# Rows of the split tokens: from one place modulo 256 bytes per tile to places that alternate from row to row

## The chip, the cores and the metric

The kernel runs on one core of a Trainium2 chip. A core has TensorE (matrix products; the profile's PE, with PEld for its weight loads), VectorE (DVE), ScalarE (ACT), GpSimd (POOL) and SyncE (SP, which here only issues transfers). The metric is the device time of one execution in microseconds (us), as the median of several runs. SBUF is the core's working memory: 128 partitions, in each of which a tile takes a run of bytes. A "place" below is the byte address of a row within its partition, modulo 256.

## What is computed

One layer of a decoder trunk over 4096 prompt tokens and 64 sample tokens, width 1024. Cut to what matters:

```python
h = _rmsnorm(x, g_pre)
z = h @ w_in                       # (tokens, 1024) @ (1024, 2816)
cb, cc, ch, cg, q, k, v, ag, mq, mg = _split_cols(z)
out_a = silu(cg) * cb * conv3(cc * ch)           # gated short convolution
out_b = silu(ag) * window_attention(q, k, v)     # window 128, a sink per head
out_c = silu(mg) * memory_attention(mq)          # 256 memory tokens
y = concat([out_a, out_b, out_c]) @ w_out
x = x + _rmsnorm(y, g_post)
```

All in float32, and the outputs also hold the new keys, values and convolution states. The change concerns the product `h @ w_in` alone.

## The kernel before, in words

The kernel has two long stages: the input projection (to about 917 us), then attention, output projection and the last norm, block by block.

**The input projection.** The 4160 tokens go in 8 blocks of 2 x 260 tokens (`HW = 260`). Three phases (`PHASES`) take 4, 4 and 3 pairs of 128-column groups of `w_in`, and in each phase all blocks run through. In the first phase the two first blocks (`PLAIN_BLOCKS`) are computed directly, in 8 steps; all others by a Strassen-Winograd scheme of 7 products per pair (`PRODUCTS`), each on a token operand (B.., T..) and a weight operand (A.., S..) that are sums of quarters. A token operand is a tile of 128 partitions x 4 rows (`KH = 4`, the parts of the contraction) x 260 tokens.

**Splitting.** TensorE multiplies in a reduced form of float32 (`F32R`), so every operand is split into a rounded part and the rest: `split` (line 363 on ScalarE, line 364 on VectorE) makes `hi` and `lo` of a token operand, `x_split` does so for the plain blocks, `w_split` for the weights, which lie as `w[:, 0]` and `w[:, 1]` in one tile of 2 x 512 columns.

**The product.** `product` (line 373) runs 12 matmuls of 128 x 260 into one PSUM bank: for each of the 4 rows k, `hi[k]` with the weights' first half, `lo[k]` with the same weights, `hi[k]` with the second half. The token row is the moving operand, the 128 x 128 piece of weights is loaded before each matmul. The sequence of moving rows is thus hi, lo, hi, then hi, lo, hi of the next row. The result is moved out of PSUM by `evict` (VectorE, ScalarE), and the `finish_...` functions store it to DRAM for the second stage.

**Where the split tiles lie.** `hi` and `lo` have two buffers each, from one pool `hp`, made after the pool `hx` of the unsplit operands. A tile has 4 rows of `XR = 320` elements of 4 bytes, 1280 bytes, five times 256; 260 of the 320 are used, from element 48 on in `hi` and from element 16 on in `lo` (`begins`). As the program is built, the `lo` buffers begin at 131680 and 136800, the `hi` buffers at 141920 and 147040. So every used row of `lo` lies at place 160 and every row of `hi` at place 32. The pieces of weights lie at place 224, all of them.

**What sets the order.** In the first stage the program fixes the order of work by hand on every engine (`manual_schedule`); the order doesn't depend on where tiles lie. When the second stage opens (`open_attention`), the pools of the first are closed and their bytes are given to new tiles; whoever first writes such a tile waits for the last user of the bytes.

Of the kernel before, what the change touches and what calls it, by code (L numbers as in the profile page):

```python
# [8 lines left out]
F32 = mybir.dt.float32  # L9
F32R = mybir.dt.float32r  # L10
# [5 lines left out]
P = 128  # L16
D = 1024
KT = D // P
KH = KT // 2
# [2 lines left out]
NB = 8  # L22
NT = 4096 + NS
HW = 260
XR = 320
NBLK = NT // (2 * HW)
CT = 256
NCH = 4096 // CT
# [19 lines left out]
def f(ap):  # L48
    return ap.bitcast(F32)
# [3 lines left out]
def hybrid_layer(ctx: ExitStack, tc: tile.TileContext, a: dict):  # L53
# [31 lines left out]
    pa = ExitStack()  # L85
# [2 lines left out]
    psa = ExitStack()  # L88

    place = ctx.enter_context(tc.tile_pool(name="place", bufs=1)).tile([P, 2, KH, HW], F32, name="place")  # L90
    hxp = pa.enter_context(tc.tile_pool(name="hx", bufs=4))
    hp = pa.enter_context(tc.tile_pool(name="hp", bufs=2))
    own = ExitStack()
    kept_z = ExitStack()
    zp, used = {}, {1: [], 2: []}
# [37 lines left out]
    def accumulator(i, w, name):  # L133

        tag = "xy"[i % 2]
        if pa1 is None:
            return pa2[tag].tile([P, 2, 512], F32, tag=tag, name=name)
        return pa1[tag, w].tile([P, w, 512], F32, tag="c", name=name)
# [212 lines left out]
                tc.keep_in_program_order(ins)  # L351
            store(hd[b][o], ops[o])

    begins = {"hi": 48, "lo": 16}

    def split_tile(tag, name):

        n = begins[tag]
        return hp.tile([P, KH, XR], F32R, tag=tag, name=name)[:, :, n : n + HW]

    def split(src, name):
        hi, lo = split_tile("hi", f"hi{name}"), split_tile("lo", f"lo{name}")
        S.copy(hi, src)
        V.tensor_tensor(lo, src, f(hi), op=ALU.subtract)
        return hi, lo
# [216 lines left out]
    def x_split(b, o, meanwhile=lambda: None):  # L582
        x = xs[0, b][o]
        h0[b, o] = hi, lo = [split_tile(n, f"{n}0_{b}{o}") for n in ("hi", "lo")]
        for k in range(KH):
            if k == 1:
                meanwhile()
            g = gain_of(o, k)
            S.mul(hi[:, k], x[:, k], g)
            V.scalar_tensor_tensor(lo[:, k], x[:, k], g, f(hi[:, k]), op0=ALU.mult, op1=ALU.subtract)  # L590
# [112 lines left out]
    x_of(0, 0, "B21")  # L703

    idle = accumulator(1, 2, "idle")
    warm = hp.tile([P, KH, XR], F32R, tag="lo", name="warm").rearrange("p k n -> p (k n)")
    G.memset(f(warm[:, : P + 512]), 1.0)
    for n in (416, 416, 416, 416, 512, 512, 512, 416):
        TE.matmul(idle[:, 0, :n], warm[:, :P], warm[:, P : P + n], start=True, stop=True)
# [980 lines left out]
```

## Time and profile before

| | |
|---|---|
| time, median of 3 runs | 1530.43 us (1530.04 to 1531.11) |
| the profiled execution | 1529.03 us, span 1527.3 us |
| matmuls of the input projection, line 373 | to about 917 us |
| attention and output projection | from about 917 us on |
| DMA, mean over the span | 201 GB/s, 306.28 MB |

The profile is one execution. Its page gives busy times by engine, the chain of work that ended last, and groups of instructions by source line; other views list the busy time in chosen stretches, the waits, and the instructions in order of time. Two things are to be kept in mind. A matmul's end is modelled and matmuls overlap, so the mean duration of a row is not the distance from one to the next; that distance is found by counting matmuls in a stretch without waits. And a few matmul records can be missing, so counts come from the code where they matter.

### The profile page before, as it was taken

What the parts mean: (1) busy time and instruction counts of PE and PEld (TensorE: products, weight loads), DVE (VectorE), ACT (ScalarE), POOL (GpSimd) and SP (SyncE); (2) the same over time, 40 slices, a digit from 0 to 9 for tenths busy, and PEclk for the clock granted to TensorE, in tenths of its full rate; (3) what the DMA queues carried; (4) which work ended last, traced back from release to release, by engine and by line L of the source; (5) the groups of instructions that cost most, each with busy time, mean ns of one, the idle gap of its engine ahead of it and who ended that gap; (6) DMA issues with size and microseconds to landing.
All of it is one profiled execution on the core that took longest, in us unless ns stands there. A gap on an engine that the chain in (4) does not pass through costs nothing.

```text
span 1527.3 us, 30150 instructions
## 1 busy us (share of the span) xinstructions
PE 1514.2 (99%) x11331; PEld 1391.6 (91%) x11331; DVE 1145.1 (75%) x2055; ACT 806.2 (53%) x2039; POOL 381.0 (25%) x604
## 2 busy tenths in 40 slices
PE   9999999999999999999999999999999999999998
PEld 9999999999999999999999998788888888888876
DVE  6778888899887777997677678766666666666743
ACT  7776666576222222445455457656655565565632
POOL 0222333221300000000101204544444444444310
PEclk9999999999999999999999999999999999999999
DMA  9989999878755333778877789977777777776333
GB/s 274 200 213 242 286 277 259 301 238 273 194 182 181 127 127 127 240 231 278 243 262 224 242 286 259 226 160 149 149 148 152 162 149 158 162 155 145 131 110 97
DMA packets 177943, 306.28 MB, mean 201 GB/s; under 512 B 33926, under 2 KB 107654, under 8 KB 177766
## 3 DMA queue, kind: packets, MB, share of 16 engines
q1 hardware_dynamic: 130901, 227.38, 48.2%
q0 software_dynamic: 46176, 75.92, 24.9%
q8 instruction: 90, 1.47, 0.4%
q10 hardware_dynamic: 720, 1.05, 0.2%
q14 instruction: 56, 0.45, 0.1%
HBM read 197.23 MB, written 108.05 MB: 200 GB/s over the span
## 4 chain that ended last, share of the span: by engine, by line
PE 87%; DVE 5%; issue 4%; DMA 2%; POOL 1%; ACT 1%; SPq 0%; ACTq 0%; POOLq 0%; DVEq 0%
PE c L373 47%; PE y L1499 23%; PE ws L1253 4%; PE wo L1095 2%; PE wt L1276 2%; PE xs L1189 2%; PE xt L1204 2%; PE wo L1225 2%; PE wo L1231 1%; PE mem_acc L796 1%; DVE z L380 1%; DMA ws10A<-in_w_in 1%; DMA vd<-v 1%; DMA place<-hd_B 0%; DMA ws20A<-in_w_in 0%
## 5 line engine op out<-in xcount | busy, mean ns | idle before, releaser
L1499 PE MATMUL y<-wo,mh 128*128 128x512 f32 (+1 forms) x1040 | 350.1, 399 | 0.0
L380 DVE TENSOR_TENSOR z<-c,z 128x520 f32<-128x520 f32 (+1 forms) x308 | 194.8, 647 | 80.7 <-PE c L373 79.0
L1499 PEld LDWEIGHTS y<-wo,mh 128*128 128x128 f32 x1040 | 194.3, 188 | 39.3 <-issue 2.4
L1499 PE MATMUL y<-wo,ml 128*128 128x512 f32 (+1 forms) x520 | 201.8, 388 | 0.0
L1266 ACT ACTIVATE sm<-sm,wnm 128x128 f32<-128x128 f32 x256 | 99.5, 390 | 60.9 <-DVE wnm L1260 60.0
L1198 POOL TENSOR_SCALAR xp<-xp,xrd 128x256 f32<-128x256 f32 x128 | 74.6, 590 | 208.0 <-DVE xrd L1194 207.1
L1499 PEld LDWEIGHTS y<-wo,ml 128*128 128x128 f32 x520 | 98.2, 189 | 16.2
L1190 DVE TENSOR_REDUCE xmx<-xs 128x2 f32<-128x512 f32 x64 | 44.1, 689 | 59.3 <-PE xs L1189 59.2
L1278 ACT COPY wpt<-wt 128x512 f32<-128x512 f32 x64 | 37.2, 582 | 87.7 <-PE wt L1276 85.2
L1253 PEld LDWEIGHTS ws<-kst,q 128*128 128x128 f32 x512 | 70.0, 190 | 5.4 <-ACT xp L1193 0.7
L1506 DVE TENSOR_TENSOR yn<-y,gpost 128x512 f32<-128x512 f32 (+1 forms) x66 | 45.1, 684 | 39.6 <-PE y L1499 39.3
L1253 PE MATMUL ws<-kst,q 128*128 128x256 f32 x512 | 73.1, 283 | 0.4 <-ACT xp L1193 0.4
L1507 ACT ACTIVATE y<-y 128x512 f32<-128x512 f32 (+1 forms) x66 | 38.5, 584 | 64.2 <-DVE yn L1506 64.2
L744 POOL CAST wmask<-negs 128x256 uint8<-128x256 f32 x1 | 0.8, 822 | 265.2 <-ACT z L382 265.2
L1286 POOL TENSOR_SCALAR_AFFINE_SELECT wpt<-wpt 128x512 f32<-128x512 f32 x64 | 52.7, 823 | 42.0 <-ACT wpt L1278 39.1
L1193 ACT ACTIVATE xp<-xs,xnm 128x256 f32<-128x256 f32 x128 | 58.9, 464 | 7.1 <-DVE xnm L1191 7.1
L1128 POOL DMA_DIRECT2D q<-qd x64 | 42.8, 674 | 70.2 <-DMA qd<-zh 60.2
L1117 POOL DMA_DIRECT2D kst<-qd x64 | 38.7, 617 | 63.7 <-PE xt L1204 41.5
L1517 DVE SCALAR_TENSOR_TENSOR xr<-yn,yst,xr 128x1024 f32<-128x1024 f32 (+2 forms) x34 | 43.1, 1269 | 14.6 <-POOL yst L1513 13.2
L1256 DVE COPY_PREDICATED sm<-wmask,ws 128x256 f32<-128x256 uint8 x124 | 52.1, 436 | 2.4 <-ACT sm L1255 2.0
L1283 POOL TENSOR_SCALAR_AFFINE_SELECT wpv<-wpt 128x512 f32<-128x512 f32 x62 | 40.5, 653 | 50.6 <-ACT wpt L1278 50.5
L275 ACT ACTIVATE nat<-nat 104x1024 f32<-104x1024 f32 x40 | 42.3, 1057 | 18.5 <-DMA nat<-in_x_p 18.5
(962 smaller groups left out, 5076.2 us busy)
## 6 DMA issues: line engine op xcount, KB each, us to landing
q<-qd POOLq DMA_DIRECT2D x64, 384.0 KB, 8.3
xr<-in_x_p SPq DMA_DIRECT2D x32, 512.0 KB
nat<-in_x_p SPq DMA_DIRECT2D x39, 416.0 KB
o_yp<-xr SPq DMA_DIRECT2D x31, 512.0 KB
md<-th POOLq DMA_DIRECT2D x48, 260.0 KB, 7.2
qd<-zh SPq DMA_DIRECT2D x48, 260.0 KB
qd<-z SPq DMA_DIRECT2D x48, 260.0 KB
kst<-qd POOLq DMA_DIRECT2D x60, 192.0 KB, 5.5
```

Of the source, the lines that this page charges most:

```text
L373: TE.matmul(bank[:, :HW], l, r, start=first and i == 0, stop=last and i == 3 * KH - 1)
L380: add = lambda dst, other: V.tensor_tensor(dst, c, other, op=ALU.add)
L1190: V.tensor_reduce(mx[:, :nb], s, axis=AX.X, op=ALU.max)
L1193: S.activation(p[:, i, :], s[:, i, :], AF.Exp, bias=nm[:, i : i + 1], scale=SCALE, accum_out=den[:, i : i + 1])
L1198: G.tensor_scalar(p[:, i, :], p[:, i, :], rd[:, i : i + 1], 0.5, op0=ALU.mult, op1=ALU.mult)
L1253: TE.matmul(s3[:, hh, :], self.q[:, 4 + 2 * (2 * half + hh) + kvh, i * P : i * P + P], self.kst[:, 2 * kvh + part, i * P : i * P + 2 * P], ...
L1256: V.copy_predicated(sm[:, 2 * half : 2 * half + 2, :], third["wmask"], third["negs"] if first else s3[:, :, 0:P])
L1266: S.activation(sm[:, hh, :], sm[:, hh, :], AF.Exp, bias=nm[:, hh : hh + 1], scale=SCALE, accum_out=den[:, hh : hh + 1])
L1286: G.affine_select(p3, p3, pattern=[[0, 4], [1, P]], compare_op=ALU.is_ge, fill=0.0, base=0, channel_multiplier=-1)
L1499: TE.matmul(acc, self.hl[l][:, k], wo[k][c0 // 512][:, r, c0 % 512 : c0 % 512 + c1 - c0], start=j == 0, stop=j == passes * KT - 1)
L1506: V.tensor_tensor(yn[:m, c0:c1], acc[:m], gpost[:m, c0:c1], op=ALU.mult)
L1517: V.scalar_tensor_tensor(self.xr[:m, cs], yn[:m, cs], st[:m, 3:4], self.xr[:m, cs], op0=ALU.mult, op1=ALU.add)
```

## The change

Rows are 288 elements apart in place of 320, 1152 bytes, which is four and a half times 256. `hi` and `lo` get a pool each, `lo` first, and two small tiles that nothing uses (64 and 128 bytes) stand ahead of them. The rows begin at the start of the tile.

```diff
-XR = 320
+XR = 288
...
+    pads = [0]
+
+    def pad(where, n):
+
+        pads[0] += 1
+        where.enter_context(tc.tile_pool(name=f"pad{pads[0]}", bufs=1)).tile([P, n], F32, name=f"pad{pads[0]}")
+
     hxp = pa.enter_context(tc.tile_pool(name="hx", bufs=4))
-    hp = pa.enter_context(tc.tile_pool(name="hp", bufs=2))
+    pad(pa, 16)
+    hp = {"lo": pa.enter_context(tc.tile_pool(name="hplo", bufs=2))}
+    pad(pa, 32)
+    hp["hi"] = pa.enter_context(tc.tile_pool(name="hphi", bufs=2))
...
-    begins = {"hi": 48, "lo": 16}
-
     def split_tile(tag, name):
 
-        n = begins[tag]
-        return hp.tile([P, KH, XR], F32R, tag=tag, name=name)[:, :, n : n + HW]
+        return hp[tag].tile([P, KH, XR], F32R, tag=tag, name=name)[:, :, :HW]
...
-    warm = hp.tile([P, KH, XR], F32R, tag="lo", name="warm").rearrange("p k n -> p (k n)")
+    warm = hp["lo"].tile([P, KH, XR], F32R, tag="lo", name="warm").rearrange("p k n -> p (k n)")
```

As the program is built, the `lo` buffers begin at 131744 and 136352 (place 160) and the `hi` buffers at 141088 and 145696 (place 32). The places of the moving rows in one product are then:

| k, matmul | before | after |
|---|---|---|
| 0: hi, lo, hi | 32, 160, 32 | 32, 160, 32 |
| 1: hi, lo, hi | 32, 160, 32 | 160, 32, 160 |
| 2: hi, lo, hi | 32, 160, 32 | 32, 160, 32 |
| 3: hi, lo, hi | 32, 160, 32 | 160, 32, 160 |

Every engine has the same instructions in the same order as before. The tiles that lie behind the split tiles in the first stage (z tiles, temporaries, row factors) come to lie 1856 bytes lower or, in the second and third phase, elsewhere by a similar amount, at other places modulo 256; the weights and the tiles of the second stage stay. At the opening of the second stage the waits for released bytes change for a few instructions: the first writers of the tiles over the former place of z tiles wait for partly other stores of the projection's last block.

## The prediction

> **What bounds the kernel.** I read the page's busy shares first, then the windows view by stage, then the waits of TensorE, then the matmul rows of one undisturbed stretch.
>
> ```profile
> PE 1514.2 (99%) x11331; PEld 1391.6 (91%) x11331; DVE 1145.1 (75%) x2055; ACT 806.2 (53%) x2039; POOL 381.0 (25%) x604
> PEclk9999999999999999999999999999999999999999
> PE c L373 47%; PE y L1499 23%; PE ws L1253 4%; PE wo L1095 2%; PE wt L1276 2%; PE xs L1189 2%; PE xt L1204 2%; PE wo L1225 2%; PE wo L1231 1%; PE mem_acc L796 1%; DVE z L380 1%; DMA ws10A<-in_w_in 1%; DMA vd<-v 1%; DMA place<-hd_B 0%; DMA ws20A<-in_w_in 0%
> ```
>
> TensorE is busy 99% of the span at full granted clock, and the chain that ended last runs mostly through its matmuls: first those of line 373, the only ones the change touches. The windows view (stretch, its length, then busy time and count of PE, PEld, DVE, ACT, POOL, clock, DMA share, GB/s) and the waits of PE and PEld show how tight that is:
>
> ```profile
> 112.00:343.00 231.00, 231.00 (x1964) 231.00 (x1962) 201.94 (x251) 144.23 (x252) 65.22 (x107) 1.00 0.93 265
> 343.00:640.00 297.00, 294.44 (x2490) 293.40 (x2489) 246.19 (x336) 98.55 (x130) 20.49 (x20) 1.00 0.54 176
> 640.00:917.00 277.00, 277.00 (x2281) 270.98 (x2281) 210.14 (x334) 135.78 (x245) 22.30 (x34) 1.00 0.79 256
> PE idle L709 <- POOL warm L707: 2.2, 1, 2.2
> PE c L373 <- DVE lo_2T L364: 0.9, 2, 0.5
> PE c L373 <- DVE lo_3T L364: 0.9, 1, 0.9
> PE c L373 <- DVE lo_0B L364: 0.7, 1, 0.7
> PE c L373 <- ACT hi_3T L363: 0.2, 1, 0.2
> PE c L373 <- DVE lo_0T L364: 0.2, 1, 0.2
> ```
>
> Up to 917 us, where the products of line 373 end, line 373 waits 2.9 us in all (0.9 + 0.9 + 0.7 + 0.2 + 0.2). VectorE has 29 us to spare in the first of these stretches (231.00 - 201.94) and 51 us in the second. So what a matmul of line 373 gains or loses in spacing arrives almost whole at the end of the span. The question is only whether the spacing changes.
>
> **How the matmuls are spaced.** The code issues 64 + 168 + 224 + 168 = 624 products (two plain blocks of 8 x 4, six of 7 x 4, eight of 7 x 4, eight of 7 x 3) of 12 matmuls each: 7488. The first row below is the windows view of PE alone over 140 us without a wait; the others are line 373 in 12 us of the same stretch (minimum/median/maximum in ns).
>
> ```profile
> 480.00:620.00 140.00, 140.00 (x1191) 1.00 0.34 118
> L373 PE MATMUL c<-hi_5B,w_1A x16: 281/282/282, 540.5 to 547.5; 128*128 128x260 f32 x16
> L373 PE MATMUL c<-hi_5B,w_2A x16: 281/282/282, 541.9 to 548.9; 128*128 128x260 f32 x16
> L373 PE MATMUL c<-lo_5B,w_1A x8: 277/278/278, 540.7 to 547.4; 128*128 128x260 f32 x8
> L373 PE MATMUL c<-lo_5B,w_2A x8: 277/278/278, 542.1 to 548.8; 128*128 128x260 f32 x8
> ```
>
> The 1191 matmuls that touch the window started within 140.28 us (it also catches those begun up to 0.28 us earlier): **117.8 ns** from start to start. The rows' durations overlap, and run about 163 ns above the spacing, so differences between them stand for differences in spacing to within a nanosecond or so. Every row is 128x260, weights are 128x128 throughout, and yet a matmul on `hi` lasts 282 ns and one on `lo` 278. Two things differ between them. One is the place: `hi` rows all start at 32 modulo 256, `lo` rows all at 160, weights always at 224. The other is the neighbour: `hi`, `lo`, `hi` and then `hi` again means that one step in three, 2496 of 7488, goes from a row to another at the same place.
>
> That columns alone don't set the spacing is seen beside it, in the page's row of the score product, whose moving rows have 256 columns and keep one place within each block:
>
> ```profile
> L1253 PE MATMUL ws<-kst,q 128*128 128x256 f32 x512 | 73.1, 283 | 0.4 <-ACT xp L1193 0.4
> 400.66 0.19 PEld L373 LDWEIGHTS c<-hi_1T,w_3S 128*128 128x128 f32 x1
> 400.78 0.28 PE L373 MATMUL c<-hi_1T,w_3S 128*128 128x260 f32 x1
> 400.78 0.19 PEld L373 LDWEIGHTS c<-hi_1T,w_0S 128*128 128x128 f32 x1
> 400.89 0.28 PE L373 MATMUL c<-hi_1T,w_0S 128*128 128x260 f32 x1
> ```
>
> Four columns fewer, 283 ns: no shorter. The timeline under it shows why that is possible: the weights for the next matmul begin to load as the current one starts, and 0.11 us later the next starts. Loading and streaming run side by side, both reading SBUF. My reading is that the two reads get into each other's way by a few ns, by an amount that depends on where the moving row lies. The row shows no collision; it is an inference from 282 against 278.
>
> **The change, part by part.** Nothing is added, removed or reordered on any engine; sizes of all operations are the same. Three things move.
>
> *Places of the split rows.* After it, of the 12 matmuls of a product 6 read at 32 and 6 at 160 (before: 8 and 4), no step stays at one place, and 12 is even, so the alternation carries on into the next product. Two ways to count:
> - If the place decides: 7488 x (8/12 - 6/12) = 1248 matmuls go from 282 to 278 ns, -1248 x 4 = **-5.0 us**.
> - If the step decides: the 2496 same-place steps go from the upper `hi` value, 282, to the mean of the other two kinds, (281 + 278) / 2 = 279.5, which is -2.5 x 2496 = **-6.2 us**. That the 282s among the `hi` rows are the same-place steps is assumed.
>
> The two share a mechanism and differ by 1.2 us; I take the middle, **-5.6 us**. The far bound of a gain: all 2496 steps reach 278, -10.0 us. The bound of a loss is the 120 ns rhythm below.
>
> *Everything behind the split tiles in SBUF* (z tiles, temporaries) moves down by up to 1856 bytes and to other places modulo 256. The DVE evictions, ACT copies and DMAs keep their shapes. Only VectorE and ScalarE rows carry this, and they have the slack named above; I take 0, between -1 and +1 us. If that slack were gone the 0.9 us waits on `lo` would grow with each block, 22 blocks by some tenths.
>
> *Waits at the opening of the attention stage.* Its tiles lie over released ones, and a few first writers, above all the copies into `xpt`, now wait for the last store of `zh` as well:
>
> ```profile
> 930.30 1.11 SPq L165 DMA_DIRECT2D qd<-zh  x1
> 941.53 0.38 ACT L1208 COPY xpt<-xt 128x256 f32<-128x256 f32 x1
> md<-th POOLq DMA_DIRECT2D x48, 260.0 KB, 7.2
> ```
>
> It is issued at 930.30 + 1.11 = 931.4; a store of the same size lands a median 7.2 us later, at 938.6, and the copy is at 941.53: 2.9 us of cover. If a shorter first stage leaves these distances alone, as it should, this costs 0; if the store took 3 us longer, up to that.
>
> **Sum.** -5.6 + 0 + 0. The profiled run took 1529.03 us for a span of 1527.3; it becomes 1523.4. It lies 1.4 below the median of the three runs, 1530.43, so I forecast the median at 1530.43 - 5.6 = **1524.8 us**.
>
> **The rivals.**
>
> *The rhythm locks at 120 ns.* Line 373 has a second steady rhythm. From 772 us on, without any wait:
>
> ```profile
> 773.02 0.28 PE L373 MATMUL c<-hi_3T,w_1S 128*128 128x260 f32 x1
> 774.46 0.28 PE L373 MATMUL c<-hi_3T,w_2S 128*128 128x260 f32 x1
> L373 PE MATMUL c<-lo_3B,w_0S x4: 281/281/281, 782.2 to 783.3; 128*128 128x260 f32 x4
> L373 PE MATMUL c<-hi_3B,w_0S x8: 282/282/284, 782.1 to 783.4; 128*128 128x260 f32 x8
> ```
>
> The first two rows are the first matmuls of two products in a row: 1.44 us for 12, 120 ns each, and in this state `lo` lasts 281. Same code, same places: which rhythm holds depends on how loading and streaming stand to each other when the stretch begins, and a stretch stays in it until a wait breaks it. It is rare now. If the new alternation makes it the one that holds everywhere, the price is 7488 x (120 - 117.8) = +16.5 us: **1546.9 us**, slower. It decides from the first steady product on. For it: the score product's 283 ns are like this state's 282 and 281, so a rhythm of this kind can hold for long. Against it: in the score product the places don't alternate, and in line 373 it is the alternating `lo` steps that are short; with more of them the short rhythm should hold better, not worse. Chance 0.18.
>
> *The place plays no part.* `lo` is also the only matmul that is followed by a load from the other half of the weight tile (`w[:, 1]`); if that makes its 278, nothing changes: **1530.4 us**. The rows can't exclude it, since role and place never come apart in this kernel. The Trainium skill speaks for this one: its page "TensorE: Matmul & The Clock Gate", in the section "Step-by-step: what each phase is for", gives TensorE two independent SBUF read ports, one for the moving operand and one for the weights, and under "Back-to-back issue gap" a spacing of N / 2.4 + 2.5 ns, in which no place occurs; by it 260 columns would take an estimated 110.8 ns and this change would do nothing. The trace's 117.8 ns, and two durations for one shape, don't agree with that spacing. Chance 0.20.
>
> *A larger gain.* All steps fall to the short value: -10.0 us, **1520.4 us**. Chance 0.07, since a step to `lo` lasts 281 today.
>
> **How the numbers follow.** Forecast 0.55, larger gain 0.07, no part 0.20, 120 ns rhythm 0.18. About 0.2%, 3 us, is what a measurement of this kernel tells from no change. Faster: 0.55 + 0.07 = 0.62; same 0.20; slower 0.18. The range takes in the far gain and the case of no change with the +1 and up to 3 us of the two small terms, 1519.5 to 1533.5; the slow rhythm, 0.18, is left out. The forecast's own range, with the step from 5.0 to 6.2 us and the small terms, is 1522 to 1527.
>
> **What would show it.** In the new profile, 480 to 620 us should hold 1197 to 1199 matmuls in place of 1191 (140.28 us / 117.2 to 117.0 ns, the spacing less 5.0 or 6.2 us / 7488). The groups of line 373 tell the reasons apart: if the place or the step decides, `hi` and `lo` rows each mix 278 with 281 or 282, and their medians no longer differ by role; if role decides, `lo` stays at 278 and `hi` at 282; if the slow rhythm holds, both lie at 281 to 284 and the window has about 1169 (140.28 us / 120 ns). The start of line 1499 should come some 5 us earlier, and the attention stage from 917 us to the end should last as long as now. A changed time in that stage, or waits of `c` on `lo` that grow over 3 us, would make the working wrong even where the total fits.

## The result, and the profile after

The changed kernel is slower. Its median is 1536.86 us (15 runs, 1534.41 to 1544.69), beside 1531.52 us of the kernel before (15 runs, 1529.17 to 1536.44). The ratio, taken over all the runs, is **1.0043, 95% interval 1.0031 to 1.0054**: 0.0043 x 1531.52 = 6.6 us lost (the two medians alone are 5.3 us apart), where 5.6 us of gain was forecast.

The profiled execution took 1537.16 us for a span of 1535.4, 8.1 us more than the span before, which is at the upper end of that interval (0.0054 x 1531.52 = 8.3). The first three lines are of the page (busy times, granted clock, chain that ended last):

```profile
PE 1522.6 (99%) x11331; PEld 1400.7 (91%) x11331; DVE 1145.3 (75%) x2055; ACT 806.6 (53%) x2039; POOL 379.3 (25%) x604
PEclk9999999999999999999999999999999999999999
PE c L380 55%; PE y L1506 23%; PE ws L1260 4%; PE wo L1102 2%; PE wt L1283 2%; PE xs L1196 2%; PE xt L1211 2%; PE wo L1232 2%; PE wo L1238 1%; PE mem_acc L803 1%; DMA qd<-z 1%; DMA xr<-in_x_p 0%; DMA ws20A<-in_w_in 0%; DVE z L387 0%; DVE wo L195 0%
```

Line 373 is now line 380, and line 1499 is 1506. TensorE is busy 8.4 us longer (1522.6 - 1514.2) with as many instructions at the same clock; VectorE, ScalarE and GpSimd kept their busy times within 2 us. What is lost is lost inside TensorE's own work. The windows view (stretch, its length, busy time and count of PE, PEld, DVE, ACT and POOL, clock, DMA share, GB/s), cut at the end of the first stage, and the output product by source line (minimum/median/maximum in ns, first and last start) say in which stage:

```profile
0.00:923.00 923.00, 918.90 (x7605) 910.76 (x7606) 738.98 (x1047) 459.94 (x786) 128.72 (x198) 1.00 0.76 228
923.00:1535.40 612.40, 603.71 (x3729) 489.89 (x3727) 406.30 (x1010) 346.66 (x1255) 250.56 (x406) 1.00 0.71 157
L1506 PE MATMUL y<-wo,mh x1040: 277/393/504, 931.3 to 1528.9; 128*128 128x512 f32 x168, 128*128 128x256 f32 x6
```

The same view of the kernel before has its first output product at 924.0 us and its last at 1520.8. So the first comes 7.3 us later, and from the first to the last it is 597.6 us now and 596.8 before: about 0.8 us of the 8.1 lies in the second stage, the rest in the first. The other profiles have 595.9 to 598.6 us for the same stretch, so that 0.8 us is no more than these differ among themselves. Two windows without a wait, PE alone, before and then after, show the spacing:

```profile
490.00:620.00 130.00, 130.00 (x1106) 1.00 0.32 112
490.00:620.00 130.00, 130.00 (x1096) 1.00 0.33 116
```

Ten matmuls fewer in the same time: 130.28 us / 1106 = 117.8 ns before, 130.28 us / 1096 = **118.9 ns** after (the 0.28 us are those begun ahead of the window that still touch it). Without rounding, the difference is 1.07 ns, and 1.07 ns x 7488 matmuls = 8.0 us, about as much as the spans differ by. The waits of TensorE up to 922 us (total us, times, longest) added nothing:

```profile
PE idle L716 <- POOL warm L714: 2.2, 1, 2.2
PE c L380 <- DVE lo_3T L371: 0.9, 1, 0.9
PE c L380 <- ACT w_0A L191: 0.3, 1, 0.3
PE c L380 <- ACT hi_3T L370: 0.3, 1, 0.3
PE c L380 <- DVE lo_2T L371: 0.2, 1, 0.2
PE c L380 <- DVE lo_0T L371: 0.2, 1, 0.2
```

Line 380 waits 1.9 us, 1.0 us less than before, so that some 7 us arrive at the end of the first stage, and the 0.8 us of the second come on top. The rows of line 380 in a quiet stretch (name, count, minimum/median/maximum in ns, first and last start):

```profile
L380 PE MATMUL c<-hi_5T,w_0S x16: 282/282/284, 561.0 to 568.0; 128*128 128x260 f32 x16
L380 PE MATMUL c<-hi_5T,w_1S x16: 282/282/284, 562.4 to 569.4; 128*128 128x260 f32 x16
L380 PE MATMUL c<-lo_5T,w_0S x8: 277/280/281, 561.1 to 567.9; 128*128 128x260 f32 x8
L380 PE MATMUL c<-lo_5T,w_1S x8: 277/280/281, 562.5 to 569.3; 128*128 128x260 f32 x8
```

The reader is to see that no row became shorter. Half of the `hi` rows now lie at place 160, where 278 ns had been read, and none of them lasts 278. The median of 280 on `lo` is a mix of two values: record by record, the `lo` rows that still lie at 160 went up from 278 to 281, and those that came to 32 last 277 or 278.

The opening of the second stage kept its cover. The timeline has the last store of `zh` before the first copies, and the source view has the copies:

```profile
938.25 0.55 SPq L175 DMA_DIRECT2D qd<-zh  x1
L1215 ACT COPY xpt<-xt x9: 344/373/417, 948.8 to 1005.8; 128x256 f32<-128x256 f32 x9
```

Issued by 938.8, the store would land at an estimated 946.0 by the 7.2 us of the prediction; the first copy comes at 948.8, 2.8 us later, beside 2.9 us of cover before.

A finer reading than the window is used from here on: the time from the first matmul of one product to the first of the next, from the start times in the trace, which are whole ns. Of the 586 products that are directly followed by another, 533 took 1413 or 1414 ns before; after, 541 took 1426 or 1427. Of the others before, 18 took 1440 or 1441. The starts within one product follow each other so (ns, one product in the stretch of the windows above):

```
before   118 116 119 118 116 119 119 115 120 118 116 119   = 1413
after    121 118 119 119 116 120 121 118 119 120 115 120   = 1426
```

Before, a pattern of three matmuls repeats; after, one of six, although the places repeat every two.

### The profile page after: what moved, and what is told of

It reads as the page before. It is cut to its first block, busy times and chain, and to the rows that moved or that the text cites. A ratio compares the mean times of both kernels' runs of the same rounds, so it can differ in the third digit from the quotient of the medians.

```text
span 1535.4 us, 30148 instructions
## 1 busy us (share of the span) xinstructions
PE 1522.6 (99%) x11331; PEld 1400.7 (91%) x11331; DVE 1145.3 (75%) x2055; ACT 806.6 (53%) x2039; POOL 379.3 (25%) x604
## 4 chain that ended last, share of the span: by engine, by line
PE 93%; DVE 3%; DMA 2%; issue 1%; ACT 0%; POOL 0%; SPq 0%; DVEq 0%; POOLq 0%; ACTq 0%
PE c L380 55%; PE y L1506 23%; PE ws L1260 4%; PE wo L1102 2%; PE wt L1283 2%; PE xs L1196 2%; PE xt L1211 2%; PE wo L1232 2%; PE wo L1238 1%; PE mem_acc L803 1%; DMA qd<-z 1%; DMA xr<-in_x_p 0%; DMA ws20A<-in_w_in 0%; DVE z L387 0%; DVE wo L195 0%
## 5 line engine op out<-in xcount | busy, mean ns | idle before, releaser
L387 DVE TENSOR_TENSOR z<-c,z 128x520 f32<-128x520 f32 (+1 forms) x308 | 194.7, 646 | 88.1 <-PE c L380 86.7
L389 ACT COPY z<-c 128x520 f32<-128x520 f32 (+1 forms) x44 | 24.3, 553 | 52.1 <-PE c L380 46.9
```

Source lines behind the costliest of these rows:

```text
L387: add = lambda dst, other: V.tensor_tensor(dst, c, other, op=ALU.add)
```

## The experiments

All matmuls, and their order, are the same in every kernel; what differs is where rows or weights lie. "Distance" below is the place of a moving row less the place of its weights, modulo 256. The kernel before has the distances 64, 192, 64 for `hi`, `lo`, `hi`; the changed one alternates 64 and 192.

At first there were two theories, which the expectations call A and B: A, that the place of a row decides how long its matmul holds TensorE, and B, that the steps between the places of successive rows do.

**All rows at place 160** (e1, made from the kernel before):

```diff
-    begins = {"hi": 48, "lo": 16}
+    begins = {"hi": 16, "lo": 16}
```

> The kernel before with `hi` rows moved to place 160 too, so that no step between moving rows changes its place. Theory A (the place of the row against the weights at 224 sets a matmul's cost, 160 being the cheap one): every matmul becomes like `lo`, 278 ns, spacing below 116.5 ns, time about 1518 to 1522 us. Theory B (the rhythm: a step is short only where the chain of steps breaks a repetition; equal places fall into the 120 ns rhythm of the score product): spacing 120.0 ns, about 1547 us.

Measured: median 1548.43 us, ratio 1.0086 (1.0062 to 1.0110). PE in the window of 490 to 620 us, and rows of line 373 by source:

```profile
490.00:620.00 130.00, 130.00 (x1086) 1.00 0.36 127
L373 PE MATMUL c<-hi_5T,w_2S x16: 281/282/283, 570.4 to 577.5; 128*128 128x260 f32 x16
L373 PE MATMUL c<-lo_5T,w_2S x8: 285/285/285, 570.5 to 577.3; 128*128 128x260 f32 x8
```

The spacing is 130.28 us / 1086 = 120.0 ns. The `lo` rows did not move at all; they lie at 160 as before, and went from 278 to 285 ns, the longest of all. So 278 was no property of place 160. A falls; the spacing and the time are those that B gave.

**`hi` and `lo` exchange their places** (e2, from the kernel before: `hi` at 160, `lo` at 32):

```diff
-    begins = {"hi": 48, "lo": 16}
+    begins = {"hi": 16, "lo": 48}
```

> The kernel before with the places of `hi` and `lo` exchanged: 160, 32, 160 in each row. Theory A: two matmuls in three are cheap instead of one, spacing about 117.1 ns, time about 1525 us. Theory B: only the sequence of steps counts, and it is the same up to a shift of 128: spacing 117.8 ns, time as before.

Measured: 1549.19 us, ratio 1.0101 (1.0087 to 1.0115).

```profile
490.00:620.00 130.00, 130.00 (x1079) 1.00 0.36 126
L373 PE MATMUL c<-hi_5T,w_1S x15: 281/284/289, 569.9 to 576.8; 128*128 128x260 f32 x15
L373 PE MATMUL c<-lo_5T,w_1S x8: 277/281/282, 569.8 to 576.7; 128*128 128x260 f32 x8
```

120.7 ns. The steps between places are those of the kernel before with the two places exchanged, two of three to another place and one to the same, and the spacing rose by 2.9 ns. So B as stated falls too: something beside the rows themselves counts, and what stayed where it was is the weights.

**The rows back, all else kept** (e3, from the changed kernel: pools of their own and unused tiles stay; the z tiles and temporaries lie 192 bytes higher than in the kernel before, where the change has them 1856 lower, which is the same place modulo 256):

```diff
-XR = 288
+XR = 320
```

> The changed kernel with rows 320 elements apart again, so the matmul rows are back at 32, 160, 32, while the pads, the two pools and the shift of what lies behind stay (now 192 bytes higher than in the kernel before). If the places of the rows are the cause of the loss: spacing 117.8 ns and time as before, within 0.2%. If the pools or the tiles behind are: 118.9 ns and about 0.4% slower.

Measured: 1534.21 us beside 1534.49 before, ratio 0.9994 (0.9981 to 1.0007).

```profile
490.00:620.00 130.00, 130.00 (x1106) 1.00 0.33 116
L380 PE MATMUL c<-hi_5T,w_0S x16: 281/282/282, 560.6 to 567.6; 128*128 128x260 f32 x16
L380 PE MATMUL c<-lo_5T,w_0S x8: 277/278/278, 560.7 to 567.4; 128*128 128x260 f32 x8
```

The count and the rows of the kernel before are back. The places of the rows are the cause, and all the rest of the change costs nothing that can be measured.

**Everything 32 bytes further** (e4, from the kernel before, a 32-byte tile ahead of the pools of weights on either side of SBUF):

```diff
+    ctx.enter_context(tc.tile_pool(name="padl", bufs=1)).tile([P, 8], F32, name="padl")
+    ctx.enter_context(tc.tile_pool(name="padr", bufs=1, side="right")).tile([P, 8], F32, name="padr")
     wa = ctx.enter_context(tc.tile_pool(name="wa", bufs=3 * NP_))
```

> The kernel before with 32 unused bytes ahead of the weight pools on both sides, so that weights, token rows and most tiles of the second stage start at a multiple of 64 bytes instead of 32 past one; steps between rows stay as they are. If the extra time per matmul comes from rows that straddle 64-byte pieces (the totals of a product, 1413, 1427 and 1440 ns, differ by 13.3, two times 6.67 ns, which would be the time of such a piece): the 512-column product of the second stage drops by up to 6.7 ns per matmul (1592 of them, -10 us) and line 373 shortens as well. If only differences between places count: no change.

Measured: 1537.11 us, ratio 1.0020 (1.0008 to 1.0033). The left side grows upwards and the right side downwards, so this did a little more than its name says. The rows came to 64 and 192 and the weights of pairs 0 to 2 to 0, all at their old distances; the weights of pair 3, on the right, came to 192, at the distances 128, 0, 128. PE in the window, rows by source, and the group of the output product:

```profile
490.00:620.00 130.00, 130.00 (x1100) 1.00 0.33 116
L375 PE MATMUL c<-hi_5B,w_0S x8: 281/282/283, 572.1 to 573.4; 128*128 128x260 f32 x8
L375 PE MATMUL c<-hi_5B,w_2S x8: 281/282/282, 574.9 to 576.2; 128*128 128x260 f32 x8
L375 PE MATMUL c<-hi_5B,w_3S x8: 277/283/288, 576.3 to 577.7; 128*128 128x260 f32 x8
L1501 PE MATMUL y<-wo,mh 128*128 128x512 f32 (+1 forms) x1040 | 351.2, 400 | 0.0
```

This is the clearest single run. The same token rows are read in all of these, a few us apart. With weights at the old distance a product takes 1413 to 1416 ns (419 of 472), with those of pair 3 it takes 1443 or 1444 (110 of 114), 120.25 ns a matmul. (3 x 117.8 + 120.25) / 4 = 118.4 ns, which is the window's 130.28 us / 1100. A boundary of 64 bytes that rows or weights could straddle has nothing to do with it: pairs 0 to 2 moved by 32 bytes and kept their time, and the output product's mean is 400 ns (399 in the kernel before).

**Block by block through the pairs of places** (e5, e6, e7, one run each; from the kernel before, rows 1280 bytes apart, places for `hi` and `lo` taken from a list with one pair per block, 8 x 8 pairs in all, two of them twice):

```diff
-    def split_tile(tag, name):
+    SWEEP = [(2, 6), (1, 4), (6, 4), (0, 3), (2, 3),
...
-        n = begins[tag]
+        n = begins[tag] if at is None else 8 * SWEEP[(-PLAIN_BLOCKS, 6, 14)[at[0]] + at[1]][tag == "lo"]
```

> The kernel before, but each of the 22 blocks of the input projection after the plain ones places its `hi` and `lo` rows at another pair out of 8 x 8 places, 32 bytes apart modulo 256; 22 pairs here. The spacing is read block by block in stretches without waits. If only the places relative to the weights count (theory B as it now stands), the pair (160, 32), place of `hi` first, gives 120.7 ns as in the run with exchanged places, (160, 160) gives 120.0, every other pair of equal places 120.0 too, and no product lies off the 6.67 ns grid by pair. If a different rhythm can be had, some pair lies under 117.8 ns. If the place of a row counted by itself, the blocks would fall into rows and columns by place.

> As the first sweep, 22 further pairs of places. Equal places: 120.0 ns by theory B. If neighbours of the pair of the kernel before, (32, 160), are as fast, the rhythm hangs on 64 bytes or more; if all others are at 120 or above, the kernel before sits at a narrow best.

> As the first sweep, the last 20 pairs, and in the last two blocks (32, 160), which should give 117.8 ns, and (160, 160), which should give 120.0. (32, 160) also stands in the second block: the same 117.8 there if a block's spacing hangs on its own pair and not on what ran before.

Measured: 1543.56, 1539.94 and 1553.71 us beside 1538.30 before. From the product starts of each block (places, median over its products of the ns for one matmul; a choice of the 64 pairs):

```
hi    lo            hi    lo             hi    lo
32    160  117.8    64    224  118.9     160   32   121.0
224   192  117.8    128   64   118.9     96    160  122.2
224   32   117.8    0     32   118.9     192   160  122.2
192   224  117.8    96    32   118.9     64    96   122.2
```

All eight pairs of equal places run at 120.0, and 120.0 is the median of the 64. No place has a value of its own: `hi` at 96 comes to between 118.9 and 122.2 ns, by where `lo` lies. The pair of e2, (160, 32), was expected at 120.7; its products go round 120.1, 121.1 and 121.0, so that 121.0 is the median and 120.7 the mean, as in e2. The repeats agree: 117.8 for (32, 160) twice, 120.0 for (160, 160) twice. The pair (96, 224) has the distances 128 and 0, those of pair 3 in e4, and gives 120.2 ns (there 120.25), though neither rows nor weights lie where they lay there. The kernel before sits on one of four pairs that reach the lowest value.

**Rows at other distances from one another** (e8, e9, one run each; from the kernel before, the list changed for every operand: rows 1152, 1216, 1088, 1184 or 1120 bytes apart, each with many pairs of places):

```diff
+    SWEEP = [(288, 48, 56), (304, 32, 24), (288, 48, 0), (304, 8, 40), (288, 0, 48),
...
+        return t.rearrange("p k n -> p (k n)")[:, n : n + KH * r].rearrange("p (k n) -> p k n", k=KH)[:, :, :HW]
```

> The kernel before, with the places changed from product step to product step (48 matmuls each, the last 24 are read): all 64 pairs of places with rows 1152 bytes apart (the row step of the change, +128 modulo 256), and 34 pairs with rows 1216 bytes apart (-64); in the third phase 56 pairs with 1184 (-96). If a changing place from row to row is bad in itself, because the pattern takes more matmuls to close, all 64 pairs of the first family lie at 118.9 ns or above, with the pair of the changed kernel, (32, 160), at 118.9. If only this pair is bad, some of the family lie at 117.8 or below, as 4 of the 64 pairs without a row step do. A pair under 117.8 would be a layout better than both kernels.

> As the run before it, with rows 1088 bytes apart (+64, 64 pairs), the other 30 pairs of 1216, four repeats, and in the third phase 56 pairs with 1120 (+96). Of the repeats, the layout of the kernel before should show 117.8 ns, that of the change 118.9 wherever it stands. If the best any family reaches is 117.8, that is a floor for this product, 53 units of 6.67 ns for three matmuls.

Measured: 1542.80 and 1544.01 us beside 1529.54 before. With rows 1152 bytes apart, as in the change, `hi` from 32 and `lo` from 160 gives 118.9 ns in both runs, the changed kernel's value; two of 64 pairs reach 117.8, (96, 128) and (224, 0); the median is 120.0 and the worst 123.3. Of the other four distances one pair came clearly below 118.9: `hi` from 192 and `lo` from 0 with rows 1120 bytes apart, two products of 1420 ns, 118.3 ns; none came to 117.8. Of the some 370 readings in the five runs none is below 117.75. One pair, (160, 32), gave 118.9 in one stretch and 120.0 in another: places narrow down the rhythm, but how a stretch begins also chooses.

**The change with another pair of places** (e10, from the changed kernel; the rows are still 1152 bytes apart and alternate, `hi` from 96, `lo` from 128):

```diff
-    pad(pa, 16)
+    pad(pa, 8)
...
-    pad(pa, 32)
+    pad(pa, 56)
```

> The changed kernel with other unused bytes ahead of the two pools (32 and 224 in place of 64 and 128), so that `hi` rows start at place 96 and `lo` rows at 128; rows stay 1152 bytes apart, so every place still changes by 128 from row to row. In the sweep this pair ran at 117.8 ns. If the loss of the change comes from which places the rows take, 117.8 ns everywhere and the time of the kernel before within 0.3%; if it comes from the alternation, 118.9 ns or more and at least 0.4% slower.

Measured: 1530.12 us beside 1532.01 before, ratio 0.9992 (0.9978 to 1.0005).

```profile
490.00:620.00 130.00, 130.00 (x1106) 1.00 0.32 112
```

117.8 ns, in a pattern of six (120, 120, 118, 116, 117, 116). So alternating places are not bad in themselves; the changed kernel's pair is. Nor are they better than rows that keep their place: the spacing is that of the kernel before. (What lies behind the split tiles is 1792 bytes lower here, nearly as far as in the changed kernel.)

**The weights moved, the rows left** (e11, from the kernel before; the weights go by 128 bytes to place 96, and `begins` takes back the rows' own shift, so that they stay at 32, 160, 32):

```diff
+    ctx.enter_context(tc.tile_pool(name="padl", bufs=1)).tile([P, 32], F32, name="padl")
+    ctx.enter_context(tc.tile_pool(name="padr", bufs=1, side="right")).tile([P, 32], F32, name="padr")
...
-    begins = {"hi": 48, "lo": 16}
+    begins = {"hi": 16, "lo": 48}
```

> The kernel before with the weights' tiles moved by 128 bytes, to place 96, and the token rows kept at 32, 160, 32. If the load of the weights and the moving rows get into each other's way, the distance between the two is what counts, and this is the run with exchanged places over again: 120.7 ns, about 1% slower. If only the token rows' places and steps count: 117.8 ns and no change. The second stage's products move all their operands by 128 together and should not change.

Measured: 1548.08 us, ratio 1.0107 (1.0092 to 1.0123).

```profile
490.00:620.00 130.00, 130.00 (x1079) 1.00 0.35 123
L375 PE MATMUL c<-hi_5T,w_3S x16: 281/284/289, 565.0 to 572.1; 128*128 128x260 f32 x16
L375 PE MATMUL c<-lo_5T,w_0S x12: 278/281/282, 560.8 to 573.5; 128*128 128x260 f32 x12
```

Count and row durations of e2 (1079, 284, 281), whose distances these are: 192, 64, 192. The rows lie where they lay before. That the spacing depends on how the rows lie to the weights is hereby shown, and not only argued.

The spacings account for the times. The 586 products, with the waits inside them, sum to 835.0 us before and 842.9 after, 7.9 us apart. On the chip of e1 to e4 the layout of the kernel before is seen in e3, 840.4 us (50 of its products came at 120 ns, 33 of them in a row from 8 to 55 us: the same places have two rhythms); e1 has 853.3 and e2 854.6, 12.9 and 14.2 us more, beside 13.2 and 15.5 us from the ratios.

## Why the prediction was wrong

**What bounds the kernel: right.** "What a matmul of line 373 gains or loses in spacing arrives almost whole at the end of the span." Of some 8 us of spacing, 7.3 us stand at the first output product, and the waits that became 1.0 us shorter account for the rest.

**The places of the split rows: wrong, and this is the step that failed.** The prediction read 282 ns on `hi` and 278 on `lo` and carried the 4 ns, as a property of the place or of the step, to another sequence of places. The reading itself was right (within one row k the three matmuls last 281, 278 and 282 ns, and the 282 is the one before a step to the same place, as was assumed), but the durations are not portable. They belong to one steady rhythm, which all rows of the repeating pattern set together by their distances to the weights. e1 shows it best: rows that nobody touched went from 278 to 285 because their neighbours moved. The change exchanged a rhythm of 353.3 ns for three matmuls (a quarter of 1413.3) for one of 713.3 ns for six (half of 1426.7), 117.8 for 118.9 ns each. The two counts of the prediction, -5.0 and -6.2 us, differed little because both rested on this one assumption; that they agreed said nothing of its truth. The signs that the prediction named say so too. `hi` and `lo` were each to mix 278 with 281 or 282; `lo` does, but with 281 at place 160 and 278 at 32, and `hi` has 282 and 284. The window of 480 to 620 was to hold 1197 to 1199 matmuls. (It has 1169, but that stretch includes an idle gap now, and the 1169 are no sign of a 120 ns rhythm; 490 to 620 is free of it.)

**What lies behind the split tiles: right, as far as can be measured.** It was put at 0, between -1 and +1 us. e3 has these tiles at the places of the change modulo 256 and is at 0.9994, -2.9 to +1.1 us by its interval. VectorE's slack was not used up:

```profile
L387 DVE TENSOR_TENSOR z<-c,z 128x520 f32<-128x520 f32 (+1 forms) x308 | 194.7, 646 | 88.1 <-PE c L380 86.7
```

This is the group of `evict` in the changed kernel (busy us, mean ns, idle before and its releaser): VectorE waits 86.7 us for line 380.

**The waits at the opening of the second stage: right,** 0 to 3 us, with no cost seen (cover of an estimated 2.8 beside 2.9 us; e10, whose z tiles lie nearly as low as in the changed kernel, takes the time of the kernel before).

**The rivals.** The 120 ns rhythm had the right sign and the right kind of mechanism, a steady rhythm that line 380 stays in, but not the right rhythm: 118.9 ns, and 6.6 us lost in place of 16.5. It does exist as the prediction said: in e3 the places of the kernel before run at 120.0 ns for 33 products, `lo` at 281. e1 has the same spacing throughout, with `lo` at 285, so 120.0 ns is the total of more than one pattern. The argument against it, that more steps to `lo`'s kind must help, fell with the result, and e2 says why: with as many alternating steps as the kernel before it loses 1.0%, so such steps are not short in themselves. That the place plays no part falls: e1, e2 and e11 change nothing but places and lose 0.9 to 1.1%. The rule that the prediction cited for it, from the Trainium skill ("TensorE: Matmul & The Clock Gate", "Step-by-step: what each phase is for"), was that the moving operand and the weights come in through independent read ports; e11 does not agree with independence, since 128 bytes on the weights' side alone cost 2.9 ns a matmul. The spacing of N / 2.4 + 2.5 ns, which the prediction took from the same page of the Trainium skill ("Back-to-back issue gap"), is given there for an isolated matmul; for a stream with weight loads the section says that both operations set the spacing, so it was not the rule for line 373. The larger gain did not come, and e5 to e10 found none by places, with weights at 224 and rows at multiples of 32 bytes: 117.8 ns is the least that any of them showed, and the kernel before is already there.

**Open.** That the load of the weights and the reading of the row get in each other's way is the reading that fits e11; no row shows such a collision, and why one distance costs and another does not was not found. The four best pairs of e5 to e7 have the distances (64, 192), (0, 224), (0, 64) and (224, 0), and no rule was found that fits these and forecasts the rest. Nor is it settled why one layout can have two rhythms, as (160, 32) has in e8 and e9 and that of the kernel before in e3.

## What to carry to other kernels

A difference between two groups of back-to-back matmuls is a symptom of the pattern they stand in and can't be multiplied by a new count of their kinds; when places change, the spacing has to be measured anew, for the whole repeating sequence and against where the weights lie. Before a layout is changed for such a difference, put all rows at one place and exchange two places: two edits of one line show whether the duration goes with the place at all. And count starts in a window without waits, since the rows' own durations (277 to 289 ns here) hide a loss of 1.1 ns in each of 7488.

## What the hardware showed that was not expected

- **A grid of 6.67 ns.** In the kernel before, the changed kernel and e1, products of 12 take 1413.3, 1426.7 and 1440.0 ns on the mean: 212, 214 and 216 units of 6.67 ns. Three matmuls take 53 units before and 54 in e1, six take 107 after the change.
- **The rhythm can be longer than the layout's.** In e2 the places repeat every three matmuls, the starts only every nine (124, 117, 125, 118, 116, 120, 127, 120, 120 ns). The changed kernel's places repeat every two matmuls and its `hi`, `lo`, `hi` every three, its starts every six; the short step of 115 or 116 ns stands at another position of the product in other stretches.
- **How much hangs on places.** 120.0 ns is the common value, for all eight pairs of equal places too; unequal places can reach 117.8 or cost 122.2 ns (e5 to e7), a range of 4.4 ns a matmul, or an estimated 33 us over 7488, that no instruction count shows.
